# A later spread of two roots, another half-tile for twelve SwiGLU results, and a crossed order of blocks in two paired units

## The chip, the cores and the metric

The kernel runs on one core of one Trainium2 chip. The metric is the device time of one execution, in microseconds (us). The kernel before takes 1804.71 us, the median of 3 runs (1804.05 to 1805.07).

## What is computed

A trunk of two residual layers over 1024 positions of 1024 channels, in float32, conditioned by one vector `c`. Layer 0 mixes tokens with a causal convolution, layer 1 with trailing means over 2, 4, 8 and 16 positions. Behind each mixer stands a dense SwiGLU with 2816 hidden channels. Cut to what matters here:

```
for i in range(2):
    sh_m, sc_m, g_m, sh_f, sc_f, g_f = split(silu(c) @ ada_w[i] + ada_b[i], 6)
    h = rms_norm(x, norm_mix_g[i]) * (1 + sc_m) + sh_m
    x = x + (1 + g_m) * mixer_i(h)
    h = rms_norm(x, norm_ffn_g[i]) * (1 + sc_f) + sh_f
    x = x + (1 + g_f) * ((silu(h @ w_gate) * (h @ w_up)) @ w_down)
return rms_norm(x, final_g)
```

`rms_norm(x, g)` is `x * rsqrt(mean(x*x over channels) + 1e-6) * g`.

## The kernel before

**Layout.** Channels lie on the 128 partitions (8 tiles `x_0` to `x_7`), positions along the free dimension. The sequence is cut in two chunks of 512 positions, A and B. Their stages alternate, so that one chunk's norms and mixers lie beside the other's matrix products: layer 0's SwiGLU of A, then of B, then layer 1's of A, then of B.

**Products.** TensorE (PE) works with operands rounded to a shorter format. Each value is split in `hi` (a cast by ScalarE, ACT) and `lo` (the rest, a subtraction by VectorE, DVE), and each product is made of three: `hi` by the weights' `hi`, `lo` by `hi`, `hi` by `lo`. So a 1024-channel product of one hidden tile takes 8 x 3 matmuls. `hhi` and `hlo` are the parts of the normed input `h`; `ghi` and `glo` of the SwiGLU result; `thi` and `tlo` of sums of halves of `h` (below). Weights come as `raw` from memory, ACT makes the `hi` and, for some, DVE the `lo`.

**The order of the work.** A planner written in Python emits the program: it goes through a list of units (matrix work), keeps an estimated `clock` of each engine, and between them lets tasks take steps on the other engines. PE's order is what the planner emitted; the order on the other engines is then set by a scheduler that sees the whole program. A task that waits for an answer says so: `mean_rsqrt` (line 458) says "stats", issues 4 small products `var` (column sums of the squares over all channels), 12 small DVE steps for 1/sqrt, says "spread", and issues 4 products `rstd` that copy the row of roots onto all partitions. Then ACT copies the result to `ny`, DVE makes `t = x * gain * ny` for the 8 channel tiles, ACT makes `hhi` of each and DVE `hlo`. Behind "stats" and "spread" the planner leaves a number of microseconds by its clock (`DELAY`, line 62: 2.75 and 1.5 for urgent tasks) in which it emits matrix work of others. The norm ahead of layer 1's SwiGLU is the task "nf" (in `pooled`): chunk A's is placed in the last units of B's layer 0, chunk B's in the last units of A's layer 1. `Squares` beside it collects the squares.

**The paired units.** Most hidden tiles go in pairs, by a scheme of the Strassen kind: seven blocks of 12 products of 256 positions in place of eight (`ffn_pair`, line 1144). The blocks are named by their weights: `w11`, `w12`, `w22` as they are, `s1` to `s4` sums of them (the `shi`, `slo` of the rows below; each made by DVE or GpSimd and ACT in the slots of the weights). `w11`, `s2`, `s3` and `w22` accumulate one behind the other in the left half of a bank `a`; `w12` in the left half of a bank `e`; `s1` and `s4` in its right half. Since the partial results are wanted too, ACT copies `a` behind `w11` and again behind `s2` (to `r`, left and right), and the right half of `e` behind `s1` (to `q`). So `s2` waits for the first copy, `s3` for the second, `s4` for the copy of `q`. In most pairs the blocks run `w11, s1, s2, w12, s3, s4, w22`; in the first paired unit of A's and of B's layer 1 (`plain_first`) `w12` is taken ahead of `s1`, since the sums `t` of the norm's result are made only shortly before, and the order is `w11, w12, s1, s2, s3, s4, w22`. The seven sets of the pair behind it are prepared during the unit: a set is written when the block that read its slot is done.

**Tiles for the results.** `gslots` (line 252) hands out the tiles of `ghi` and `glo`, for each of a chunk's 22 hidden tiles in each of two layers. Tiles are 512 positions of 4 bytes in slots that are 32 elements (`ALIGN`, 128 bytes) longer; one of the two parts starts at the slot's start and the other 32 elements in, by turns, as the count `ch.made` says. In all, 176 such tiles are handed out. 12 of them, `ghi` and `glo` of A's layer 1 for the hidden tiles 0, 4, 8, 12, 16 and 20, start at 192 bytes past a multiple of 256; the other 164 start at 64.

Of the kernel before, what the change touches and what calls it, by code (L numbers as in the profile page):

```python
# [18 lines left out]
S = 1024  # L19
KT = D // P  # L20
F = 2816
NF = F // P
# [36 lines left out]
UNTIL = (18, 18, 22)  # L59
OUT_AT = 5  # L60
DELAY = {"stats": 2.75, "spread": 1.5}
DELAY_BEHIND = {"stats": 8, "spread": 4}

_COLS = {}
# [51 lines left out]
def trunk(ctx, tc, xT, c, vec, ada, adan, w1, w2, wgu, wdn, wpl, wph, out):  # L116
    nc = tc.nc
    ctx.enter_context(tc.manual_schedule(engines={mybir.EngineType.PE}))
    clock = {"PE": 0.0, "V": 0.0, "G": 0.0, "S": 0.0}
    V_ = Engine(nc.vector, "V", clock, PRICES["V"], lambda i: order(i))  # L120
# [53 lines left out]
    lax = [False]  # L174
# [37 lines left out]
    class Task:  # L212


        def __init__(self, gen, urgent=False, at=None):
            self.gen, self.done, self.urgent, self.until, self.mark = gen, False, urgent, 0.0, None
            tasks.insert(0 if urgent else len(tasks) if at is None else at, self)

        def step(self, e):
            if e != "V" or self.done or clock["PE"] < self.until and not forced[0]:  # L220
                return False
            try:
                if self.mark is None:
                    self.mark = clock["PE"] - V_.spent
                said = next(self.gen)
                if said == "wait":
                    return False
                if said in LOAD:
                    self.until = clock["PE"] + LOAD[said]
                    if said == "mean":  # L230
                        self.mark = None
                elif said is not None:
                    self.until = (self.mark + V_.spent if self.urgent else max(clock["V"], clock["S"])) + (DELAY if self.urgent or not lax[0] else DELAY_BEHIND)[said]
                    self.mark = None
            except StopIteration:
                self.done = True
                tasks.remove(self)
            return True
# [12 lines left out]

    def gslots(ch):

        odd = (ch.made // (KT // 2) + ch.i) % 2
        ch.made += 1
        return [wslot(ch, name, F32R, at * ALIGN, ch.n) for name, at in (("ghi", odd), ("glo", 1 - odd))]

# [886 lines left out]
    def ffn_pair(ch, l, me, following, downs, later, plain_first=False):  # L1144


        def emit(take):
            wt = take()
            wt.prepare()
            ws = wt.made  # L1150
            h, T = st["h", ch.i], st["T", ch.i]
            half = KT // 2
            b11 = [(hi[:, LEFT], lo[:, LEFT]) for hi, lo in h[:half]]
            b21 = [(hi[:, LEFT], lo[:, LEFT]) for hi, lo in h[half:]]
            b22 = [(hi[:, RIGHT], lo[:, RIGHT]) for hi, lo in h[half:]]
# [12 lines left out]
            left, right = e[:, LEFT], e[:, RIGHT]  # L1168
            r, q = temp(ch.n), temp(ch.n)
            quad(a[:, :H], w11, b11, True)  # L1170
            S_.copy(r[:, LEFT], a[:, :H])
            if plain_first:
                quad(left, w12, b21, True)
            quad(right, s1, t1, not plain_first)
            S_.copy(q[:, RIGHT], right)
            pace()
            down()
            quad(a[:, :H], s2, t2, False)
            S_.copy(r[:, RIGHT], a[:, :H])
            if following is not None and hasattr(following, "raws"):  # L1180
                following.prepare()
                st["ahead"]()
            if not plain_first:
                quad(left, w12, b21, False)
            if following is None:
                used[0] -= 2
                st["ahead"]()
            pace()
            down()
            quad(a[:, :H], s3, t3, False)  # L1190
            V_.tensor_tensor(q[:, RIGHT], q[:, RIGHT], a[:, :H], op=ADD)
            quad(right, s4, b22, False)
            V_.tensor_tensor(r, r, e, op=ADD)
            if later is not None:
                later.load(later.dps[0])
            pace()
            down()
            quad(a[:, :H], w22, t4, False)
            if me.which == 0:
                sg = st["sg", ch.i] = [window(ch.n, "sg") for _ in range(2)]  # L1200
                S_.activation(sg[0], r, AF.Silu)
                S_.activation(sg[1][:, RIGHT], q[:, RIGHT], AF.Silu, scale=-1.0)
                S_.activation(sg[1][:, LEFT], a[:, :H], AF.Silu, scale=-1.0)
            else:
                sg = st["sg", ch.i]
                V_.tensor_tensor(r, r, sg[0], op=MUL)
                V_.scalar_tensor_tensor(q[:, RIGHT], q[:, RIGHT], -1.0, sg[1][:, RIGHT], op0=MUL, op1=MUL)
                V_.scalar_tensor_tensor(q[:, LEFT], a[:, :H], -1.0, sg[1][:, LEFT], op0=MUL, op1=MUL)
                for i, t in enumerate((r, q)):
                    hi, lo = st["g", ch.i, me.f + i] = gslots(ch)  # L1210
                    S_.copy(hi, t)
                    V_.tensor_tensor(lo, t, f32(hi), op=SUB)
            pace()
            down()
            while downs is not None and downs.todo:
                downs.slot()
        return emit, (me,)
# [231 lines left out]
    st["taps", 0], st["taps", 1] = [False] * KT, [False] * KT  # L1449
    T = {}  # L1450

    def put(name, gen, urgent=False):
        def emit(take):
            T[name] = Task(gen(), urgent)
        unit(emit)

    def need(*names):
# [107 lines left out]
    def pooled(us, ch, out_at):  # L1565

        if ch.i == 0:
            ada_need((1, 0), (1, 1), (1, 2))
        put(("pool", ch.i), lambda: pool(ch))
        for i, (e, ws) in enumerate(us):  # L1570
            if i == out_at:
                need(("pool", ch.i))
                squares = Squares(ch)
                for q in range(2):
                    pool_out(ch, 1, q, squares)
                if ch.i == 0:
                    ada_need((1, 3), (1, 4), (1, 5))
                put(("nf", ch.i), lambda: norm(ch, 1, True, ("hn", ch.i), True, squares), True)
            unit(e, *ws)
        need(("nf", ch.i))  # L1580
        unit(lambda take: st.__setitem__(("h", ch.i), st["hn", ch.i]))
# [88 lines left out]
```

## Time and profile before

| | |
|---|---|
| time, median of 3 runs | 1804.71 us (1804.05 to 1805.07) |
| the profiled execution's own time | 1806.63 us |
| its span in the profile | 1804.9 us |
| mean granted TensorE clock | 0.993 |
| PE busy | 1769.9 us, 98% of the span |
| DVE, ACT and GpSimd (POOL) busy | 1401.4, 1044.5 and 549.5 us |

Times in the profile are microseconds from the start of the span. A row of a timeline gives the start, the duration, the engine, the line of the kernel, the operation, what it writes and reads (without the numbers that tell equally named tiles apart), shapes, a count, and in brackets how long the engine had been idle before and what released it. Matmuls overlap, so the distance from one start to the next says more than the duration. Since every operation is recorded by a helper, nearly all rows have the helper's line: L132 for matmuls, L110 for the other engines.

### The profile page before, as it was taken

What the parts mean: (1) busy time and instruction counts of PE and PEld (TensorE: products, weight loads), DVE (VectorE), ACT (ScalarE), POOL (GpSimd) and SP (SyncE); (2) the same over time, 40 slices, a digit from 0 to 9 for tenths busy, and PEclk for the clock granted to TensorE, in tenths of its full rate; (3) what the DMA queues carried; (4) which work ended last, traced back from release to release, by engine and by line L of the source; (5) the groups of instructions that cost most, each with busy time, mean ns of one, the idle gap of its engine ahead of it and who ended that gap; (6) DMA issues with size and microseconds to landing.
All of it is one profiled execution on the core that took longest, in us unless ns stands there. A gap on an engine that the chain in (4) does not pass through costs nothing.

```text
span 1804.9 us, 27284 instructions
## 1 busy us (share of the span) xinstructions
PE 1769.9 (98%) x10148; PEld 1536.0 (85%) x10148; DVE 1401.4 (78%) x2278; ACT 1044.5 (58%) x1682; POOL 549.5 (30%) x600
## 2 busy tenths in 40 slices
PE   9999998999999999999999999999999999999997
PEld 7777777888888888899998878999998789999996
DVE  8689846978775328989996988878769888887866
ACT  4776765776746455555556356555554556555553
POOL 0389723887734121211113501101125111011111
PEclk9999999999999999999999999999999999999998
DMA  9969676998978998877665566455555665655441
GB/s 305 283 181 264 170 168 166 238 220 209 233 205 209 233 216 201 233 203 205 201 186 146 147 155 153 129 133 140 136 128 145 166 150 137 184 141 138 127 111 57
DMA packets 113207, 322.88 MB, mean 179 GB/s; under 512 B 11057, under 2 KB 21425, under 8 KB 113074
## 3 DMA queue, kind: packets, MB, share of 16 engines
q1 hardware_dynamic: 77936, 222.56, 37.3%
q0 software_dynamic: 33984, 97.53, 30.2%
q8 instruction: 79, 1.29, 0.3%
q10 hardware_dynamic: 1154, 1.05, 0.2%
q14 instruction: 54, 0.44, 0.1%
HBM read 316.90 MB, written 4.19 MB: 178 GB/s over the span
## 4 chain that ended last, share of the span: by engine, by line
PE 88%; DVE 3%; issue 3%; DMA 2%; ACT 2%; POOL 1%; POOLq 0%; SPq 0%; DVEq 0%; ACTq 0%
PE dn L132 25%; PE up L132 24%; PE gate L132 24%; PE y L132 5%; PE a L132 3%; PE g L132 2%; PE first L132 2%; DVE x L110 1%; ACT w L110 1%; PE ada L132 1%; PE idle L132 1%; DMA w<-in_wdn_dram 1%; ACT t L110 1%; PE rstd L132 1%; DMA raw<-in_wgu_dram 0%
## 5 line engine op out<-in xcount | busy, mean ns | idle before, releaser
L132 PE MATMUL dn<-ghi,w 128*128 128x512 f32 (+1 forms) x1440 | 474.7, 388 | 0.8 <-ACT t L110 0.6
L110 ACT CAST w<-raw 128x512 fp32r<-128x512 f32 (+1 forms) x410 | 320.4, 783 | 168.4 <-PE up L132 73.3
L132 PEld LDWEIGHTS dn<-ghi,w 128*128 128x128 f32 x1440 | 269.2, 189 | 51.4 <-ACT t L110 1.0
L110 DVE SCALAR_TENSOR_TENSOR x<-dn,gains,x 128x512 f32<-128x512 f32 (+1 forms) x360 | 262.9, 736 | 63.0 <-PE dn L132 57.5
L110 ACT ACTIVATE w<-raw 128x1024 fp32r<-128x1024 f32 (+1 forms) x236 | 206.9, 877 | 172.6 <-PE dn L132 50.2
L1095 POOL DMA_DIRECT2D w<-in_wgu_dram x100 | 87.0, 873 | 637.3 <-PE up L132 206.1
L132 PE MATMUL dn<-glo,w 128*128 128x512 f32 (+1 forms) x720 | 279.4, 388 | 0.1
L132 PE MATMUL up<-hhi,w 128*128 128x512 f32 (+1 forms) x1008 | 274.9, 347 | 0.0
L132 PE MATMUL gate<-hhi,w 128*128 128x512 f32 (+1 forms) x1008 | 274.9, 347 | 0.0
L110 POOL TENSOR_TENSOR pa<-pa,pr 128x512 f32<-128x512 f32 x174 | 240.5, 1480 | 41.2 <-ACT pr L110 38.1
L132 PEld LDWEIGHTS gate<-hhi,w 128*128 128x128 f32 x1008 | 179.6, 189 | 26.0 <-PE ada L132 0.4
L132 PEld LDWEIGHTS up<-hhi,w 128*128 128x128 f32 x1008 | 179.7, 189 | 24.6
L132 PE MATMUL gate<-hlo,w 128*128 128x512 f32 (+1 forms) x504 | 175.0, 347 | 0.0
L132 PE MATMUL up<-hlo,w 128*128 128x512 f32 (+1 forms) x504 | 174.8, 347 | 0.0
L110 DVE SCALAR_TENSOR_TENSOR ca<-u,vecs,ca 128x512 f32<-128x512 f32 x246 | 171.7, 748 | 0.9
L110 DVE TENSOR_TENSOR w<-raw,w 128x512 fp32r<-128x512 f32 (+1 forms) x174 | 133.9, 775 | 31.9 <-ACT w L110 27.5
L132 PEld LDWEIGHTS dn<-glo,w 128*128 128x128 f32 x720 | 136.0, 189 | 20.9 <-POOL glo L110 0.6
L425 POOL DMA_DIRECT2D w<-in_wgu_dram x72 | 64.2, 891 | 246.7 <-ACT w L110 223.1
L110 ACT ACTIVATE pr<-u,vecs 128x512 f32<-128x512 f32 x174 | 118.4, 717 | 26.3 <-POOL pa L110 17.2
L110 DVE TENSOR_TENSOR t<-t,up 128x256 f32<-128x256 f32 (+1 forms) x88 | 53.7, 611 | 100.8 <-PE up L132 97.5
L110 ACT CAST shi<-ny 128x512 fp32r<-128x512 f32 x100 | 62.0, 620 | 119.2 <-PE gate L132 59.3
L132 PEld LDWEIGHTS gate<-hlo,w 128*128 128x128 f32 x504 | 95.2, 189 | 12.9 <-DVE hlo L110 0.2
(196 smaller groups left out, 3741.2 us busy)
## 6 DMA issues: line engine op xcount, KB each, us to landing
raw<-in_wgu_dram SPq DMA_DIRECT2D x176, 512.0 KB, 4.7
raw<-in_wdn_dram SPq DMA_DIRECT2D x88, 512.0 KB, 5.4
w<-in_wgu_dram POOLq DMA_DIRECT2D x72, 512.0 KB, 7.7
adaw<-in_ada_dram SPq DMA_DIRECT2D x64, 512.0 KB, 4.9
w<-in_wgu_dram POOLq DMA_DIRECT2D x100, 256.0 KB, 5.7
raw<-in_w_dram SPq DMA_DIRECT2D x42, 512.0 KB, 6.1
adaw<-in_adan_dram SPq DMA_DIRECT2D x32, 512.0 KB, 6.1
w<-in_w_dram POOLq DMA_DIRECT2D x32, 512.0 KB, 8.2
```

What stands on the lines that cost most here:

```text
L110: self.last = self.order(getattr(self.eng, name)(out, *args, **kw))
L132: last_mm[0] = nc.tensor.matmul(out, lhsT, rhs, start=start, stop=stop, **kw).ins.name
L425: order(nc.gpsimd.dma_start(as_src(lo), src, accum_op=ADD))
L1095: order(nc.gpsimd.dma_start(lo, src, accum_op=ADD))
```

## The change

There are three edits. In the changed kernel the helpers stand one line lower (L133, L111).

1. The task "nf" gets its own delays, `DELAY_AMONG`: "spread" is 4.2 by the planner's clock in place of 1.5.
2. In `gslots`, `turned` swaps the places of `ghi` and `glo` within their slots for the hidden tiles 0, 4, 8, ... of chunk A's layer 1. Addresses change, and no instruction or wait. With it all 176 tiles start at 64 bytes past a multiple of 256.
3. In `ffn_pair` with `plain_first`, the order of blocks is `w11, w12, s2, s1, s3, s4, w22`.

```diff
+DELAY_AMONG = {"stats": 2.75, "spread": 4.2}
...
-                    self.until = (self.mark + V_.spent if self.urgent else max(clock["V"], clock["S"])) + (DELAY if self.urgent or not lax[0] else DELAY_BEHIND)[said]
+                    self.until = (self.mark + V_.spent if self.urgent else max(clock["V"], clock["S"])) + (self.delay or (DELAY if self.urgent or not lax[0] else DELAY_BEHIND))[said]
...
-        odd = (ch.made // (KT // 2) + ch.i) % 2
+        turned = ch.i == 0 and ch.made >= NF and (ch.made - NF) % 4 == 0
+        odd = (ch.made // (KT // 2) + ch.i + turned) % 2
...
+            def crossed(first):
+                quad(right, s1, t1, first)
+                S_.copy(q[:, RIGHT], right)
+
             if plain_first:
                 quad(left, w12, b21, True)
-            quad(right, s1, t1, not plain_first)
-            S_.copy(q[:, RIGHT], right)
+            else:
+                crossed(True)
             pace()
             down()
             quad(a[:, :H], s2, t2, False)
...
-            if not plain_first:
+            if plain_first:
+                crossed(False)
+            else:
                 quad(left, w12, b21, False)
...
-                put(("nf", ch.i), lambda: norm(ch, 1, True, ("hn", ch.i), True, squares), True)
+                put(("nf", ch.i), lambda: norm(ch, 1, True, ("hn", ch.i), True, squares), True, delay=DELAY_AMONG)
```

**The root on PE.** PE's order where chunk A's "nf" spreads its root, among the last `dn` products of B's layer 0 (`dn_9901` is the second block of 6 products behind the column sums `var`). Before:

```order
L132 MATMUL dn_9901<-ghi_9644,w_9730 128x512
L132 MATMUL rstd_9909<-ident,col_9881 128x128 [waits DVE_49]
L132 MATMUL rstd_9909<-ident,col_9881 128x128 x3
L132 MATMUL dn_9948<-ghi_9407,w_9722 128x512
L132 MATMUL dn_9948<-glo_9408,w_9722 128x512
```

and in the changed kernel, where two further blocks stand ahead (`dn_9917` is the fourth) and `gate_9979` opens the next unit:

```order
L133 MATMUL dn_9917<-ghi_9644,w_9730 128x512
L133 MATMUL rstd_9925<-ident,col_9881 128x128 [waits DVE_49]
L133 MATMUL rstd_9925<-ident,col_9881 128x128 x3
L133 MATMUL dn_9964<-ghi_9407,w_9722 128x512
L133 MATMUL dn_9964<-glo_9408,w_9722 128x512
L133 MATMUL dn_9964<-ghi_9407,w_9723 128x512
L133 MATMUL dn_9964<-ghi_9644,w_9729 128x512
L133 MATMUL dn_9964<-glo_9645,w_9729 128x512
L133 MATMUL dn_9964<-ghi_9644,w_9730 128x512
L133 MATMUL gate_9979<-hhi_5913,w_9779 128x512 [waits Activation_49]
```

The spread moved from 12 to 24 products behind the column sums, and from 18 to 6 products ahead of the next unit. In B's "nf" the same two blocks of 6 change sides.

**The norm on ACT.** ACT's order from the copy of that root (`ny`) on; `hhi_9835` to `hhi_9849` are the `hi` parts of the 8 channel tiles, `w_9975` to `w_10114` steps on weights. Before:

```order
L110 COPY ny_9914<-rstd_9909 128x512 [waits PE_49]
L110 ACTIVATE hhi_9835<-t_9916,mod 128x512 [waits DVE_49]
L110 ACTIVATE hhi_9837<-t_9920,mod 128x512 [waits DVE_49]
L110 ACTIVATE w_9975<-raw_9972 128x1024 [waits PE_49]
L110 ACTIVATE hhi_9839<-t_9924,mod 128x512 [waits DVE_49]
L110 CAST w_9983<-raw_9981 128x1024 [waits DMAHW1_49,DMASW4_49,PE_49]
L110 ACTIVATE w_9984<-raw_9981 128x1024 [waits PE_49]
L110 CAST w_10045<-raw_10043 128x1024 [waits DMAHW2_49,DMASW5_49,PE_49]
L110 ACTIVATE hhi_9841<-t_9928,mod 128x512 [waits DVE_49]
```

and in the changed kernel the same stretch:

```order
L111 COPY ny_9930<-rstd_9925 128x512 [waits PE_49]
L111 ACTIVATE w_9975<-raw_9972 128x1024 [waits PE_49]
L111 CAST w_9983<-raw_9981 128x1024 [waits DMAHW1_49,DMASW4_49,PE_49]
L111 ACTIVATE w_9984<-raw_9981 128x1024 [waits PE_49]
L111 CAST w_10045<-raw_10043 128x1024 [waits DMAHW2_49,DMASW5_49,PE_49]
L111 ACTIVATE hhi_9835<-t_9932,mod 128x512 [waits DVE_49]
L111 ACTIVATE hhi_9837<-t_9936,mod 128x512 [waits DVE_49]
L111 ACTIVATE hhi_9839<-t_9940,mod 128x512 [waits DVE_49]
```

Four weight steps of 1024 columns moved ahead of the first `hhi`. Further on, `hhi_9847` and `hhi_9849` moved behind the weight step `w_10114` and the silu `t_10038` of the running unit.

**The norm on DVE.** DVE's last steps of the same norm; `hlo_9848` and `hlo_9850` belong to the seventh and eighth channel tile. Before:

```order
L110 SCALAR_TENSOR_TENSOR hlo_9846<-t_9936,mod,hhi_9845 128x512 [waits Activation_49]
L110 SCALAR_TENSOR_TENSOR hlo_9848<-t_9940,mod,hhi_9847 128x512 [waits Activation_49]
L110 TENSOR_TENSOR hf_10121<-hhi_9843,hlo_9844 128x512 [waits DVE_49]
L110 TENSOR_TENSOR hf_10160<-hhi_9837,hlo_9838 128x512
L110 SCALAR_TENSOR_TENSOR hlo_9850<-t_9944,mod,hhi_9849 128x512 [waits Activation_49]
```

and in the changed kernel:

```order
L111 SCALAR_TENSOR_TENSOR hlo_9846<-t_9952,mod,hhi_9845 128x512 [waits Activation_49]
L111 TENSOR_TENSOR w_10052<-raw_10049,w_10051 128x1024 [waits DMAHW3_49,PE_49]
L111 TENSOR_TENSOR hf_10121<-hhi_9843,hlo_9844 128x512 [waits DVE_49]
L111 TENSOR_TENSOR hf_10160<-hhi_9837,hlo_9838 128x512
L111 TENSOR_TENSOR t_10038<-t_10038,up_9980 128x512 [waits PE_49,Activation_49]
L111 SCALAR_TENSOR_TENSOR hlo_9848<-t_9956,mod,hhi_9847 128x512 [waits Activation_49]
L111 SCALAR_TENSOR_TENSOR hlo_9850<-t_9960,mod,hhi_9849 128x512 [waits Activation_49]
```

A step on weights, two sums `hf` and the multiply of the running unit's result now stand ahead of `hlo_9848`.

**The paired unit.** PE's order in A's first paired unit where the second block on bank `a` (`gate_10364`) ends and the third begins; `shi_10348` is `s2`, `shi_10354` is `s3`, `slo_10343` is of `s1`. Before:

```order
L132 MATMUL gate_10364<-thi_10298,shi_10348 128x256
L132 MATMUL gate_10364<-tlo_10299,shi_10348 128x256
L132 MATMUL gate_10364<-thi_10298,slo_10349 128x256
L132 MATMUL gate_10364<-thi_10133,shi_10354 128x256 [waits Activation_49]
L132 MATMUL gate_10364<-tlo_10134,shi_10354 128x256
```

and in the changed kernel, with bank `e` as `gate_10365`:

```order
L133 MATMUL gate_10365<-thi_10298,shi_10342 128x256
L133 MATMUL gate_10365<-tlo_10299,shi_10342 128x256
L133 MATMUL gate_10365<-thi_10298,slo_10343 128x256
L133 MATMUL gate_10364<-thi_10133,shi_10354 128x256 [waits Activation_49]
L133 MATMUL gate_10364<-tlo_10134,shi_10354 128x256
```

The block `s1` came between `s2` and `s3`. 12 products on, the first of `s4` (`gate_10365<-hhi_9843,shi_10360`) now waits for ACT too, which it did not before. On ACT the two copies change places. Before:

```order
L110 CAST shi_10432<-acc_10430 128x512 [waits PE_49,Activation_49]
L110 COPY t_10367<-gate_10365 128x256 [waits PE_49,Activation_49]
L110 CAST w_10562<-raw_10456 128x512 [waits DMAHW4_49,DMASW4_49]
L110 ACTIVATE w_10562<-raw_10456 128x512
L110 CAST shi_10438<-ny_10436 128x512 [waits PE_49]
L110 COPY t_10366<-gate_10364 128x256 [waits PE_49]
```

and in the changed kernel:

```order
L111 CAST shi_10419<-acc_10417 128x512 [waits PE_49,Activation_49]
L111 COPY t_10366<-gate_10364 128x256 [waits PE_49]
L111 CAST w_10562<-raw_10443 128x512 [waits DMAHW4_49,DMASW4_49]
L111 ACTIVATE w_10562<-raw_10443 128x512
L111 CAST shi_10425<-ny_10423 128x512 [waits PE_49]
L111 COPY t_10367<-gate_10365 128x256 [waits PE_49,Activation_49]
```

The copy of `a` (`t_10366`, the tile `r`) now goes first, and the copy of `e` (`t_10367`, `q`) four steps behind it.

More of the change, by code (lines that the diff above doesn't have):

```diff
@@ L212, in trunk, with __init__ @@
     class Task:
-        def __init__(self, gen, urgent=False, at=None):
+        def __init__(self, gen, urgent=False, at=None, delay=None):
+            self.delay = delay
             self.gen, self.done, self.urgent, self.until, self.mark = gen, False, urgent, 0.0, None
@@ L1450, in trunk, with put @@
     T = {}
-    def put(name, gen, urgent=False):
+    def put(name, gen, urgent=False, **kw):
         def emit(take):
-            T[name] = Task(gen(), urgent)
+            T[name] = Task(gen(), urgent, **kw)
         unit(emit)
```

## The prediction

> **What bounds the kernel now.** I read the page first, for the share of each engine:
>
> ```profile
> span 1804.9 us, 27284 instructions
> ...
> PE 1769.9 (98%) x10148; PEld 1536.0 (85%) x10148; DVE 1401.4 (78%) x2278; ACT 1044.5 (58%) x1682; POOL 549.5 (30%) x600
> ```
>
> PE is busy for all but 35.0 us of the span. So an edit gains only where it lets PE start sooner or makes a product shorter, and all other engines count through PE's waits. The second view is PE's waits by releaser (total, times, longest):
>
> ```profile
> PE rstd L132 <- DVE col L110: 8.3, 6, 2.5
> ...
> PE gate L132 <- ACT t L110: 2.6, 2, 1.3
> ```
>
> The first row holds the waits of the root products `rstd` for their DVE chain, 6 of them; two are those of the task "nf". The second row holds the two waits of the first paired units, 1.3 us each. The third view is PE's timeline at both.
>
> **The change part by part. The root (edit 1).** PE's timeline at A's "nf", and B's row:
>
> ```profile
> 1042.23 0.39 PE L132 MATMUL dn<-ghi,w 128*128 128x512 f32 x1
> 1042.69 1.05 PE L132 MATMUL var<-ones,acc 128*128 128x1 f32 x8
> 1043.61 0.47 PE L132 MATMUL dn<-ghi,w 128*128 128x512 f32 x1
> ...
> 1046.23 0.39 PE L132 MATMUL dn<-ghi,w 128*128 128x512 f32 x1
> 1047.94 1.16 PE L132 MATMUL rstd<-ident,col 128*128 128x128 f32 x8 [1.32 <-DVE col L110]
> ...
> 1053.05 0.39 PE L132 MATMUL gate<-hhi,w 128*128 128x512 f32 x1
> ...
> 1413.24 1.16 PE L132 MATMUL rstd<-ident,col 128*128 128x128 f32 x8 [1.32 <-DVE col L110]
> ```
>
> 12 `dn` products from 1043.61 to 1046.23 take 0.23 each after the first, so the 13th could start at 1046.46. Changing to the small fp32 products takes 0.23 more (1042.23 to 1042.69 is 0.46 for one product), so unhindered `rstd` would start at 1046.69. It starts at 1047.94: 1.25 us lost, and B's row shows the same wait. With 12 further products ahead (12 x 0.227 = 2.72) PE comes to `rstd` at 1049.41, when DVE's column has been there since about 1047.9. The wait goes, the six blocks stand all the same, and the next unit's first gate product comes at 1053.05 - 1.25 = 1051.80. Gain 1.25 at each place, 2.5 in all.
>
> What is late next: `rstd` itself is 1.47 us later (1049.41 against 1047.94), and on ACT four weight steps now stand between `ny` and the first `hhi`. ACT's and DVE's rows there:
>
> ```profile
> 1049.13 0.59 ACT L110 COPY ny<-rstd 128x512 f32<-128x512 f32 x1 [8.59 <-PE rstd L132]
> ...
> 1052.34 1.06 ACT L110 ACTIVATE w<-raw 128x1024 fp32r<-128x1024 f32 x1 [0.41 <-PE dn L132]
> 1053.31 0.70 ACT L110 ACTIVATE hhi<-t,mod 128x512 fp32r<-128x512 f32 x1
> 1053.92 1.03 ACT L110 CAST w<-raw 128x1024 fp32r<-128x1024 f32 x1
> 1054.86 1.05 ACT L110 ACTIVATE w<-raw 128x1024 fp32r<-128x1024 f32 x1
> ```
>
> ```profile
> 1053.07 0.74 DVE L110 SCALAR_TENSOR_TENSOR hlo<-t,mod,hhi 128x512 fp32r<-128x512 f32 x1
> 1053.73 0.75 DVE L110 SCALAR_TENSOR_TENSOR x<-dn,gains,x 128x512 f32<-128x512 f32 x1
> ...
> 1057.04 0.69 DVE L110 TENSOR_TENSOR hf<-hhi,hlo 128x512 f32<-128x512 f32 x1
> ...
> 1059.62 1.22 DVE L110 TENSOR_TENSOR w<-raw,w 128x1024 fp32r<-128x1024 f32 x1
> 1060.76 0.75 DVE L110 SCALAR_TENSOR_TENSOR hlo<-t,mod,hhi 128x512 fp32r<-128x512 f32 x1
> ```
>
> `ny` follows `rstd` by 1.19 us, so it starts at 1050.60 and leaves ACT at about 1051.1. Two activations at 0.97 and two casts at 0.94 are 3.82: the first `hhi` starts at 1054.92 and ends 0.70 later, at 1055.62, where it was at 1050.54 before. DVE can then do its `hlo`. By the order, DVE has from there to the seventh tile's `hlo`: 10 scalar-tensor-tensor steps at 0.66 (1053.07 to 1053.73), 4 tensor steps of 512 at about 0.60 (0.69 less the same overlap of 0.09) and 2 weight steps at 1.14 (1059.62 to 1060.76), together 11.28. So that `hlo` starts at about 1066.94 and is done at 1067.69. PE's row that reads it:
>
> ```profile
> 1068.23 0.39 PE L132 MATMUL gate<-hlo,w 128*128 128x512 f32 x1
> ```
>
> PE would come there at 1068.23 - 1.25 = 1066.98. So it waits 0.7 us, and with a slow first product behind the wait (0.11, below) loses about 0.85. The eighth tile is ready 0.66 later and PE wants it 0.68 later, so one wait covers both. Net gain 0.4 per place, 0.8 for both; the ends are 2.5 (the scheduled steps run in gaps and nothing waits) and -0.5 (DVE 0.65 us later than laid out at each place). I take 0.8, since each term is a row, and only their gaps are mine.
>
> **The crossed blocks (edit 3).** PE's timeline at A's wait, and ACT's beside it:
>
> ```profile
> 1102.07 0.28 PE L132 MATMUL gate<-tlo,shi 128*128 128x256 f32 x1
> 1102.19 0.28 PE L132 MATMUL gate<-thi,slo 128*128 128x256 f32 x1
> 1103.78 0.39 PE L132 MATMUL gate<-thi,shi 128*128 128x256 f32 x1 [1.32 <-ACT t L110]
> 1104.01 0.28 PE L132 MATMUL gate<-tlo,shi 128*128 128x256 f32 x1
> ```
>
> ```profile
> 1101.53 0.37 ACT L110 COPY t<-gate 128x256 f32<-128x256 f32 x1
> ...
> 1102.32 0.63 ACT L110 ACTIVATE w<-raw 128x512 fp32r<-128x512 f32 x1
> 1102.85 0.61 ACT L110 CAST shi<-ny 128x512 fp32r<-128x512 f32 x1
> 1103.36 0.37 ACT L110 COPY t<-gate 128x256 f32<-128x256 f32 x1
> ```
>
> Products follow each other by 0.12 (1102.07 to 1102.19), so the second product of s3 should start at 1102.43; it starts at 1104.01. 1.58 us are lost, of which 0.11 is the slow first product (0.23 to the next, not 0.12). The reason is ACT: the copy that s3 waits for is the second in its row, behind two weight steps and a cast, at 1103.36.
>
> In the changed order the copy of `a` takes the first place (1101.53, done at 1101.90), and PE comes to s3 at 1102.31: no wait. The copy of `q` takes the place at 1103.36 and is done at 1103.73. It is wanted now, by s4, 12 products behind 1102.31, at 1103.74. PE started 0.05 behind the copy's end before (1103.73 to 1103.78), so s4 loses 0.04 and a slow first product of 0.11: 0.15. Gain 1.58 - 0.15 = 1.43 at A, and the same at B by the equal wait in the second view: 2.85. Ends: 3.2 if nothing is left of the wait, and 1.8 if one more ACT cast (0.53, 1102.32 to 1102.85) comes ahead at each place.
>
> Who else waits: the multiply of the running unit, now ahead of the seventh `hlo`, reads products that end earlier than before. The sums `t` of the paired unit hang on the norm, and come about 0.5 us later on DVE. Their last row:
>
> ```profile
> 1098.07 0.69 DVE L110 TENSOR_TENSOR tlo<-tf,thi 128x512 fp32r<-128x512 f32 x1
> ```
>
> It ends at 1098.76, and s3, which reads it first, stood at 1103.78. These 5 us cover it, less the 1.5 that s3 comes sooner; past them it would cost what it is late.
>
> **The half-tiles (edit 2).** The windows of the `dn` products that read `ghi` and `glo`, PE's busy time (and number) of those products alone, in stretches where one pair's products lie:
>
> ```profile
> 1111.00:1142.00 31.00, 12.54 (x48) 1.00 0.46 121
> 1142.20:1173.50 31.30, 12.38 (x48) 1.00 0.52 141
> ...
> 1298.60:1329.40 30.80, 12.54 (x48) 1.00 0.57 143
> 1354.40:1371.10 16.70, 16.65 (x72) 1.00 0.74 184
> 1440.00:1451.30 11.30, 11.19 (x48) 1.00 0.55 121
> 988.80:1005.20 16.40, 16.35 (x72) 1.00 0.82 161
> 1074.70:1085.80 11.10, 10.99 (x48) 1.00 0.56 125
> ```
>
> A's layer 1 alternates between 12.54 and 12.38 from pair to pair, from the first window of these to the third row, four pairs at 12.54, and these are the pairs with hidden tiles 0, 4, 8 and 12, whose tiles start at 192 past a multiple of 256. The granted clock is 1.00 in all. Tiles 16 and 20 lie in the stretches of 16.65 and 11.19; the same stretches of B's layer 0, with all tiles at 64, take 16.35 and 10.99. So the start costs 4 x 0.16 + 0.30 + 0.20 = 1.14, all of it PE time. No instruction moves, so nothing hides it: gain 1.1, ends 0 and 1.15.
>
> The Trainium skill has a rule that speaks against this edit: "SBUF — State Buffer", section "SBUF: two separate sides", says that PE never waits on anyone for its port and names one contended port pair alone, that of VectorE and GpSimd; by it a start shifted by 128 bytes changes nothing here and the sum loses 1.1. The trace of before does not agree, with 12.54 against 12.38, but it cannot show that the start address is the reason.
>
> **The sum.** 0.8 + 2.85 + 1.1 = 4.75. The profiled execution of 1806.63 with a span of 1804.9 would come to 1801.9 and 1800.15. It lies 1.9 above the median; against the median I predict 1804.71 - 4.75 = 1800.0, rounded.
>
> **Rivals.**
>
> *The root's gain stays whole.* DVE would have to reach the seventh `hlo` 0.7 us sooner than laid out, for instance because its `t` steps are done while ACT has not yet made the first `hhi`, and so I count too many of them behind it. Then 2.5 in place of 0.8, 6.45 in all: 1798.3. Against it speaks that ACT's four weight steps are certain by the order. Chance 0.17.
>
> *The start address does nothing*, and the alternation has another reason. 3.65 in all: 1801.1. For it: only A's layer 1 shows it in the trace, so the tiles' start is not separated from the place in the program. Chance 0.13. The skill's rule above would have this outcome.
>
> *The wait returns at s4.* ACT's weight steps between the two copies wait for their load; if it lands 1 us late at each unit, the copy of `q` is late one for one and s4 waits. 4.75 - 2 = 2.75: 1802.0. In before the steps ran without a gap between 1101.53 and 1103.36, against it. Chance 0.12.
>
> *Slower: the late `hhi` behind a load.* On ACT the seventh and eighth `hhi` now stand behind a weight cast that waits for its own transfer. SP's row of the issue, and the page's row of such issues with the median time to landing:
>
> ```profile
> 1053.43 2.84 SPq L420 DMA_DIRECT2D raw<-in_wgu_dram  x2
> ...
> raw<-in_wgu_dram SPq DMA_DIRECT2D x176, 512.0 KB, 4.7
> ```
>
> Issued at 1053.43 it lands at about 1058. The `hhi` is wanted by DVE at 1066.94; cast (0.94), silu and `hhi` (0.6 each, by 1053.31 to 1053.92) take 2.1, so it decides from a landing after about 1064.8, and from there PE's wait grows one for one, at a product that was never waited for before. To be slower by over 0.2% (3.61 us, about what a measurement of this kernel can tell from no change) the two places have to lose 4.75 + 3.6 = 8.4 us, 4.2 each: a landing 16 us behind the issue, which gives 1808.3. Chance 0.04.
>
> **How the numbers follow.** The forecast has 0.54. The likeliest case gives 1800.0. The range reaches to the whole root gain (1798.3) with 0.3 for the upper end of edit 3, and to the wait at s4 (1802.0) with 0.3 for the lower end of the root: 1798.0 to 1802.3. Some 0.15 is left out, the slower rival and the sums of two mishaps. Faster by over 0.2% means under 1801.1. That holds for most of the forecast (0.46 of its 0.54, the rest being its upper end), for the first rival, and for half of the second: 0.46 + 0.17 + 0.07, and 0.04 for a late load of less than half a microsecond: 0.74. Same takes the rest but for the slower rival, 0.22; slower 0.04.
>
> **What would show it.** In the changed profile: no row `rstd` with a wait for `col` near 1049 and 1414; a wait of `gate` for DVE's `hlo` of about 0.7 at the seventh tile's products in each of the two units behind; `ny` some 1.5 later; no wait at s3 and one of about 0.05 at s4; `dn` windows of A's layer 1 all at 12.38, 16.35 and 11.0. Wrong would make it: a wait that is left at `rstd`, `gate` waits over 1.25 at either unit (edit 1 then costs), waits at s4 over 1 us, or `dn` windows that still alternate.

## The result and the profile after

The changed kernel takes 1800.76 us, the median of 20 runs (1797.65 to 1803.68), beside 1805.7 us for the kernel before in 20 runs on the same chips. The ratio is 0.9971, with a 95% interval of 0.9964 to 0.9977: 4.2 to 6.5 us less, 5.2 in the middle. Forecast were 4.75 less, 1800.0 us, and a range of 1798.0 to 1802.3. The profiled execution has a span of 1799.0 us, 5.9 below that of before. The page's head and the rows of PE's waits that changed:

```profile
span 1799.0 us, 27291 instructions
...
PE 1768.0 (98%) x10148; PEld 1535.9 (85%) x10148; DVE 1400.3 (78%) x2278; ACT 1043.0 (58%) x1682; POOL 549.2 (31%) x600
```

```profile
PE rstd L133 <- DVE col L111: 6.0, 4, 2.7
...
PE gate L133 <- DVE hlo L111: 1.2, 2, 0.6
```

Two waits at `rstd` are gone (4 of 6 are left, 6.0 us of 8.3). Both waits of `gate` for ACT's copy are gone from the list. A new row has come, two waits of 0.6 of `gate` for `hlo`. (The list counts idle time behind a product's modelled end, so a start that is a tenth or two late doesn't appear in it; the timelines below show those.)

**The root.** PE at A's "nf", from the column sums to the next unit:

```profile
1042.46 1.05 PE L133 MATMUL var<-ones,acc 128*128 128x1 f32 x8
1043.37 0.48 PE L133 MATMUL dn<-ghi,w 128*128 128x512 f32 x1
...
1048.71 0.39 PE L133 MATMUL dn<-ghi,w 128*128 128x512 f32 x1
1048.94 1.05 PE L133 MATMUL rstd<-ident,col 128*128 128x128 f32 x8
1049.74 0.48 PE L133 MATMUL dn<-ghi,w 128*128 128x512 f32 x1
...
1051.22 0.39 PE L133 MATMUL gate<-hhi,w 128*128 128x512 f32 x1
```

From the first `dn` to the first `gate` it is now 7.85 us, and was 9.44: 1.59 gained. `rstd` follows the last `dn` by 0.23, without any time for the change of operand. ACT and DVE behind it, and the product that has to wait:

```profile
1050.03 0.59 ACT L111 COPY ny<-rstd 128x512 f32<-128x512 f32 x1 [9.34 <-PE rstd L133]
1050.51 1.07 ACT L111 ACTIVATE w<-raw 128x1024 fp32r<-128x1024 f32 x1
1051.47 1.04 ACT L111 CAST w<-raw 128x1024 fp32r<-128x1024 f32 x1
1052.41 1.06 ACT L111 ACTIVATE w<-raw 128x1024 fp32r<-128x1024 f32 x1
1053.36 1.04 ACT L111 CAST w<-raw 128x1024 fp32r<-128x1024 f32 x1
1054.30 1.95 ACT L111 ACTIVATE hhi<-t,mod 128x512 fp32r<-128x512 f32 x3
```

```profile
1055.06 1.41 DVE L111 SCALAR_TENSOR_TENSOR hlo<-t,mod,hhi 128x512 fp32r<-128x512 f32 x2 [1.01 <-ACT hhi L111]
...
1066.37 1.41 DVE L111 SCALAR_TENSOR_TENSOR hlo<-t,mod,hhi 128x512 fp32r<-128x512 f32 x2
```

```profile
1065.96 0.61 PE L133 MATMUL gate<-hhi,w 128*128 128x512 f32 x2
1067.17 0.50 PE L133 MATMUL gate<-hlo,w 128*128 128x512 f32 x1 [0.59 <-DVE hlo L111]
1067.51 0.63 PE L133 MATMUL gate<-hhi,w 128*128 128x512 f32 x2
```

The four weight steps fill ACT from 1050.51 to 1054.30; DVE idles 1.01 us for the first `hhi`, and 11.31 us after it begins the seventh `hlo`. It is done at about 1067.1, and PE, which could have started at 1066.41, starts at 1067.17, 0.76 later (0.59 of it is idle time in the profile's count); the next product follows by 0.34 in place of 0.23. So 0.9 is lost.

**The paired unit.** PE from the end of `s1` over the end of `s3` to `s4`, and ACT's two copies with what stands between them:

```profile
1101.27 0.28 PE L133 MATMUL gate<-thi,slo 128*128 128x256 f32 x1
1101.39 0.28 PE L133 MATMUL gate<-thi,shi 128*128 128x256 f32 x1
...
1102.68 0.28 PE L133 MATMUL gate<-thi,slo 128*128 128x256 f32 x1
1102.87 0.39 PE L133 MATMUL gate<-hhi,shi 128*128 128x256 f32 x1
1103.09 0.28 PE L133 MATMUL gate<-hlo,shi 128*128 128x256 f32 x1
```

```profile
1100.62 0.36 ACT L111 COPY t<-gate 128x256 f32<-128x256 f32 x1
1100.88 0.62 ACT L111 CAST w<-raw 128x512 fp32r<-128x512 f32 x1
...
1101.93 0.61 ACT L111 CAST shi<-ny 128x512 fp32r<-128x512 f32 x1
1102.44 0.37 ACT L111 COPY t<-gate 128x256 f32<-128x256 f32 x1
```

No product in `s3` comes out of step. The first of `s4` starts 0.19 behind its forerunner and its successor 0.22 behind it, where the step is 0.12: 0.17 lost. The copy of `q` ends at 1102.81 and PE starts 0.06 later. At B the first of `s4` starts 0.25 behind its forerunner (1465.11 to 1465.36), so a little more is lost there.

**The `dn` windows** of A's layer 1, in the columns of before:

```profile
1108.00:1139.00 31.00, 12.38 (x48) 1.00 0.47 127
1139.20:1170.50 31.30, 12.38 (x48) 1.00 0.52 140
...
1295.60:1326.40 30.80, 12.39 (x48) 1.00 0.57 145
1351.20:1367.90 16.70, 16.26 (x72) 1.00 0.76 186
1436.50:1447.90 11.40, 10.87 (x48) 1.00 0.54 116
```

The alternation is gone; the seven windows of pairs lie at 12.38 or 12.39.

**Where the time went.** PE's starts of the same products in the two traces, subtracted, give the gain of each stretch. The table has them for all profiles of this study, each against that of before (negative is sooner; "t" is the start in the trace of before):

| stretch (t of its ends) | changed | e1 | e2 | e3 | e4 | e5 | e6 | e7 | e8 | e9 | e10 |
|---|---|---|---|---|---|---|---|---|---|---|---|
| start to layer 0's SwiGLU (0 to 300.1) | 0.16 | -1.30 | -1.44 | -1.43 | -0.39 | 2.15 | -2.53 | -1.91 | 1.68 | 1.53 | 1.07 |
| layer 0, no edit (300.1 to 1010.6) | -0.02 | 0.03 | -0.02 | 0.03 | 0.04 | 4.44 | 0.01 | 0.01 | -0.03 | 0.00 | -0.01 |
| A's root (1042.69 to 1069.37) | -0.70 | -0.70 | -0.03 | -0.04 | -1.40 | -0.60 | -0.72 | -1.34 | -0.07 | -0.69 | -1.37 |
| A's paired unit (1096.57 to 1108.17) | -1.41 | 0.01 | 0.18 | -1.23 | -1.37 | -1.39 | -1.30 | -1.11 | -0.46 | -1.19 | -1.21 |
| A's pairs, `dn` (1111.04 to 1371.03) | -0.74 | 0.00 | -0.73 | 0.02 | -0.74 | 0.25 | 0.59 | -0.73 | 0.00 | -0.51 | -0.74 |
| B's root (1408.03 to 1434.67) | -0.69 | -0.67 | 0.04 | 0.03 | -1.36 | -0.54 | -0.57 | -1.33 | 0.03 | -0.67 | -1.37 |
| A's last `dn` (1434.67 to 1451.24) | -0.25 | 0.02 | -0.25 | 0.01 | -0.26 | 0.06 | 0.01 | -0.22 | 0.00 | -0.25 | -0.25 |
| B's paired unit (1451.24 to 1473.74) | -1.38 | 0.00 | 0.10 | -1.42 | -1.44 | -1.43 | -1.27 | -1.31 | -0.46 | -1.40 | -1.33 |
| B's other pairs, no edit (1473.74 to 1786.38) | -0.04 | -0.04 | -0.01 | 0.02 | -0.04 | 1.12 | -0.04 | -0.04 | -0.01 | -0.04 | -0.04 |

The six stretches of the edits give 5.17 for the changed kernel. The rest of the 5.9 is no part of the change. One piece, 0.37 between 1010.61 and 1042.69, is a wait of 0.26 with its slow restart, for a transfer, that the profile of before has (`dn` for `w<-in_wdn_dram`) and none of the eleven others, those without an edit there included. The other, 0.46, is how fast one row of `rstd` products near the end went by (1.01 us from 1792.33 to the next product in before, 0.55 in the changed kernel), which differs between two profiles of one kernel (0.00 in e4, 0.47 in e10). The first row shows what a single time is worth here: up to 2.5 us either way before any edit, so the effects of single edits are read from the stretches. These have a scatter of their own: "changed" and e9, two profiles of one kernel, differ by up to 0.23 in them.

### The profile page after: what moved, and what is told of

Same layout as the page of the kernel before. It is cut to its first block, busy times and chain, and to the rows that moved or that the text cites. A ratio compares the mean times of both kernels' runs of the same rounds, so it can differ in the third digit from the quotient of the medians.

```text
span 1799.0 us, 27291 instructions
## 1 busy us (share of the span) xinstructions
PE 1768.0 (98%) x10148; PEld 1535.9 (85%) x10148; DVE 1400.3 (78%) x2278; ACT 1043.0 (58%) x1682; POOL 549.2 (31%) x600
## 4 chain that ended last, share of the span: by engine, by line
PE 91%; DVE 3%; issue 2%; ACT 2%; DMA 1%; POOL 1%; POOLq 0%; SPq 0%; ACTq 0%; DVEq 0%
PE dn L133 26%; PE up L133 25%; PE gate L133 24%; PE y L133 5%; PE a L133 3%; PE g L133 2%; PE first L133 2%; ACT w L111 1%; PE ada L133 1%; PE idle L133 1%; DVE t L111 1%; DVE hlo L111 1%; PE rstd L133 1%; DVE x L111 1%; DMA adaw<-in_adan_dram 1%
## 5 line engine op out<-in xcount | busy, mean ns | idle before, releaser
L133 PE MATMUL dn<-ghi,w 128*128 128x512 f32 (+1 forms) x1440 | 474.2, 387 | 0.6 <-ACT t L111 0.6
L111 ACT CAST w<-raw 128x512 fp32r<-128x512 f32 (+1 forms) x410 | 320.4, 783 | 170.0 <-PE up L133 72.9
L133 PEld LDWEIGHTS dn<-ghi,w 128*128 128x128 f32 x1440 | 269.4, 189 | 50.5 <-ACT t L111 1.0
L111 DVE SCALAR_TENSOR_TENSOR x<-dn,gains,x 128x512 f32<-128x512 f32 (+1 forms) x360 | 262.3, 734 | 63.8 <-PE dn L133 56.5
L111 ACT ACTIVATE w<-raw 128x1024 fp32r<-128x1024 f32 (+1 forms) x236 | 206.9, 877 | 170.9 <-PE dn L133 49.3
L133 PE MATMUL dn<-glo,w 128*128 128x512 f32 (+1 forms) x720 | 279.3, 388 | 0.1
L133 PE MATMUL up<-hhi,w 128*128 128x512 f32 (+1 forms) x1008 | 275.1, 347 | 0.0
L133 PE MATMUL gate<-hhi,w 128*128 128x512 f32 (+1 forms) x1008 | 275.0, 348 | 0.0
L111 POOL TENSOR_TENSOR pa<-pa,pr 128x512 f32<-128x512 f32 x174 | 240.6, 1481 | 41.2 <-ACT pr L111 38.1
L133 PEld LDWEIGHTS gate<-hhi,w 128*128 128x128 f32 x1008 | 179.7, 189 | 25.7 <-ACT hhi L111 0.4
L133 PEld LDWEIGHTS up<-hhi,w 128*128 128x128 f32 x1008 | 179.8, 189 | 24.5
L133 PE MATMUL gate<-hlo,w 128*128 128x512 f32 (+1 forms) x504 | 175.3, 348 | 1.2 <-DVE hlo L111 1.2
L133 PE MATMUL up<-hlo,w 128*128 128x512 f32 (+1 forms) x504 | 175.0, 347 | 0.0
L111 DVE SCALAR_TENSOR_TENSOR ca<-u,vecs,ca 128x512 f32<-128x512 f32 x246 | 171.6, 746 | 0.9
L111 DVE TENSOR_TENSOR w<-raw,w 128x512 fp32r<-128x512 f32 (+1 forms) x174 | 133.6, 773 | 32.0 <-ACT w L111 27.5
L133 PEld LDWEIGHTS dn<-glo,w 128*128 128x128 f32 x720 | 136.1, 189 | 20.4 <-POOL glo L111 0.6
L111 ACT ACTIVATE pr<-u,vecs 128x512 f32<-128x512 f32 x174 | 118.4, 717 | 26.3 <-POOL pa L111 17.2
L111 ACT CAST shi<-ny 128x512 fp32r<-128x512 f32 x100 | 62.0, 620 | 119.9 <-PE gate L133 59.7
L111 DVE TENSOR_TENSOR t<-t,up 128x256 f32<-128x256 f32 (+1 forms) x88 | 53.6, 609 | 99.6 <-PE up L133 96.4
L133 PEld LDWEIGHTS gate<-hlo,w 128*128 128x128 f32 x504 | 95.3, 189 | 15.0 <-DVE hlo L111 2.2
```

Source lines behind the costliest of these rows:

```text
L111: self.last = self.order(getattr(self.eng, name)(out, *args, **kw))
L133: last_mm[0] = nc.tensor.matmul(out, lhsT, rhs, start=start, stop=stop, **kw).ins.name
```

## Experiments

**e1, e2, e3: each edit alone**, that is the kernel before with one part of the diff.

> Edit 1 alone (the root spread 24 products behind its sums; tiles and block order as before). Theory (the terms add, each has its own place): the wait at rstd goes at both places, which moves the next unit 1.6 us forward; the seventh tile's hlo is late by 0.6 on DVE and costs 0.9 with the slow product behind it; net 0.7 at each place, 1.4 in all, ratio to before 0.9992. Rival (the new wait comes from the three edits together): no wait of gate for hlo, 3.2 us gained, ratio 0.9982. The waits at s3 (1.3 each) and the alternation of the dn windows (12.54 and 12.38) stay.

Measured 1802.93 us in 11 runs, ratio 0.9994 (0.9984 to 1.0003), which alone doesn't tell it from no change; the stretches do, 0.70 and 0.67 at the roots and 0 elsewhere. PE's waits:

```profile
PE gate L133 <- ACT t L111: 2.7, 2, 1.3
...
PE gate L133 <- DVE hlo L111: 1.2, 2, 0.6
```

The new wait comes from edit 1 alone. The rival falls.

> Edit 2 alone (only the start addresses of 12 tiles differ from the kernel before). Theory (the start address is the cause): all four slow windows of A's layer 1 come to 12.38, and about 1.0 us is gained, ratio 0.9994. Rival (the windows changed because edits 1 and 3 moved what lies beside the products): the windows alternate as before, and the time is that of before within 0.2 us in the profile. Waits at rstd and at s3 as before.

Measured 1803.58 us in 11 runs, ratio 0.9993 (0.9984 to 1.0002). The two `dn` stretches became 0.73 and 0.25 shorter. The first two windows of pairs, which are 12.54 and 12.38 in before:

```profile
1109.00:1140.00 31.00, 12.38 (x48) 1.00 0.47 124
1140.20:1171.50 31.30, 12.38 (x48) 1.00 0.53 142
```

With not one instruction moved the first window is 0.16 shorter by its busy time, and about 0.12 by the starts of its products. The start address is the cause; the rival falls. (The wait at `s3` was 1.5 at the longest in place of 1.3; e9 below shows why it moves.)

> Edit 3 alone. Theory: s3 doesn't wait, s4 loses 0.17 to a wait of 0.05 and a slow first product; 1.4 us gained in each of the two units, 2.8 in all, ratio 0.9984. Rival (the copy of q meets the weight steps of ACT at another time when the root isn't moved): s4 waits about 0.5 or more at each unit, and 1.8 or less is gained, ratio 0.9990 or more.

Measured 1803.02 us in 11 runs, ratio 0.9984 (0.9975 to 0.9993). The units gained 1.23 and 1.42. No row of `gate` waiting for ACT is left. `s4` at A:

```profile
1101.61 0.28 PE L132 MATMUL gate<-thi,slo 128*128 128x256 f32 x1
1101.97 0.39 PE L132 MATMUL gate<-hhi,shi 128*128 128x256 f32 x1
1102.20 0.27 PE L132 MATMUL gate<-hlo,shi 128*128 128x256 f32 x1
```

Here it loses 0.35, with 0.36 and 0.23 in place of 0.12, so in this profile the copy of `q` came about 0.17 later than in the changed kernel. The theory holds, with that much play. The three ratios multiplied are 0.9971, that of all three edits together; with intervals of 0.0009 either way, the last digit is luck.

**e4: 18 products behind the sums.** The planner's delay for "spread" is cut by a third:

```diff
-DELAY_AMONG = {"stats": 2.75, "spread": 4.2}
+DELAY_AMONG = {"stats": 2.75, "spread": 2.8}
```

> All three edits, but the root is spread 18 products behind its sums in place of 24. ACT's order then has the first hhi directly behind ny, ahead of the weight steps. Theory (the late root and the four weight steps ahead of the first hhi cause the new wait): rstd comes when the column is just done and loses 0.1 to 0.3, the first hhi starts about 4 us sooner, gate doesn't wait for hlo; 0.6 better than the changed kernel at each place, 1.2 in all, 6.4 below before by the terms (5.2 for the changed kernel), ratio 0.9965. Rival (DVE's own work of 11.3 us ahead of the seventh hlo is the bound): gate still waits 0.5 or more for hlo, and the time is that of the changed kernel or above. Second rival (the column is late at 18): rstd waits over 0.5, no better than the changed kernel.

Measured 1799.04 us in 5 runs, ratio 0.9962 (0.9950 to 0.9975). PE at A's root, and ACT behind it:

```profile
1046.65 0.39 PE L133 MATMUL dn<-ghi,w 128*128 128x512 f32 x1
1047.00 1.16 PE L133 MATMUL rstd<-ident,col 128*128 128x128 f32 x8
```

```profile
1048.19 0.59 ACT L111 COPY ny<-rstd 128x512 f32<-128x512 f32 x1 [7.99 <-PE rstd L133]
1049.60 0.72 ACT L111 ACTIVATE hhi<-t,mod 128x512 fp32r<-128x512 f32 x1 [0.82 <-DVE t L111]
1050.23 1.04 ACT L111 ACTIVATE w<-raw 128x1024 fp32r<-128x1024 f32 x1
```

The column is just done: `rstd` follows by 0.35, not 0.23. The first `hhi` starts 1.4 behind `ny` (4.3 in the changed kernel), and PE's list has no row of `gate` for `hlo`. Each root is worth 1.40 and 1.36, twice the changed kernel's. The theory holds, and both rivals fall.

**e7: the weight steps behind the second `hhi`**, with the root at 24 products. Scheduling edges put each weight cast behind it:

```diff
         S_.activation(hi, t, AF.Identity, bias=sh)
+        if ffn and l == 1 and k == 1:
+            held_nf[0] = S_.last.ins.name
...
         S_.copy(hi, raw)
+        if held_nf[0] is not None:
+            tc.add_manual_dep(S_.last.ins, held_nf[0], edge, reason="behind the normed tiles")
```

> The changed kernel with the root at 24 products, but ACT's weight steps are ordered behind the second hhi of the norm. Theory (the weight steps ahead of the first hhi make the new wait): first hhi at about 1.3 behind ny in place of 4.3, the seventh hlo starts about 1.5 sooner, gate doesn't wait for it, 0.9 better than the changed kernel at each place, 1.8 in all. Rival 1 (the late root itself makes the wait): gate waits 0.5 or more for hlo as in the changed kernel. Rival 2 (the weights come late instead): a new wait of DVE or PE for w, and no gain.

Measured 1797.99 us in 4 runs, ratio 0.9951 (0.9935 to 0.9968); the stretch ahead of any edit is 2.1 better than the changed kernel's in this profile, so the roots tell: 1.34 and 1.33. ACT, and the late product at A:

```profile
1047.81 0.59 ACT L111 COPY ny<-rstd 128x512 f32<-128x512 f32 x1 [10.11 <-PE rstd L133]
1049.22 1.39 ACT L111 ACTIVATE hhi<-t,mod 128x512 fp32r<-128x512 f32 x2 [0.82 <-DVE t L111]
```

```profile
1065.01 0.50 PE L133 MATMUL gate<-hlo,w 128*128 128x512 f32 x1
1065.35 0.39 PE L133 MATMUL gate<-hhi,w 128*128 128x512 f32 x1
```

The seventh tile is in time; the eighth is 0.14 late and costs 0.26 with the slow next step. 0.64 of the 0.9 is back with the weight steps alone, at an unchanged place of the root. So they make most of the wait. The theory's 0.9 was too much, and the first rival's 0.5 and more did not come. The second rival came in small: in each of the two units DVE now waits 0.29 for a weight step of ACT (before its `w` at 1055.37 and 1417.49), where the changed kernel's DVE had no such wait in these units. That alone is more than the 0.14 by which the eighth tile is late, but the late root and the eighth tile's place behind a multiply on DVE could also make it, and this run doesn't separate them.

**e8: ACT's queue without the crossing.** The kernel before, with an edge that puts the two weight steps behind the copy of `r`:

```diff
-                low_by_dma(a22, *w22, self.srcs[1][:, BACK])
+                low_by_dma(a22, *w22, self.srcs[1][:, BACK], after_copy[0])
```

> The kernel before (none of the three edits), but in the first paired units the two weight steps that stand on ACT between the copy of q and the copy of r are ordered behind the copy of r. PE's order stays w11, w12, s1, s2, s3, s4, w22. Theory (ACT's queue is half of the wait at s3, the way from PE to ACT and back the other half, which only the crossing hides): the copy starts 0.37 behind the start of s2's last product and takes 0.37, s3 starts about 0.8 sooner at each unit, a wait of 0.5 is left; 1.6 gained in all, against 2.8 for the crossing. Rival (the queue is all of it): no wait left, 2.8 gained.

Measured 1805.31 us in 10 runs, ratio 0.9993 (0.9983 to 1.0002). The median doesn't tell it from no change; by the stretches the units gain 0.46 each. ACT, and PE's first product of `s3`:

```profile
1103.42 0.62 ACT L110 CAST shi<-ny 128x512 fp32r<-128x512 f32 x1 [0.49 <-PE gate L132]
1103.95 0.36 ACT L110 COPY t<-gate 128x256 f32<-128x256 f32 x1
```

```profile
1104.36 0.39 PE L132 MATMUL gate<-thi,shi 128*128 128x256 f32 x1 [0.86 <-ACT t L110]
```

The expected 0.8 was wrong: one more step stands ahead of the copy, the cast `shi`, which is itself released by the end of `s2` (it writes into the slot that `s2` read) and takes 0.53 in front of the copy. So of 1.58 lost, the two weight steps are 0.46, and the chain from `s2` over cast and copy back to PE is the rest. Of what was tried, only the block in between hides that. Ordering this cast behind the copy as well was not tried; by the rows it would bring `s3` up to 0.53 forward.

**e5 and e6: other starts.** e5 starts all 176 tiles at 192 past a multiple of 256; e6 starts those of A's layer 1 for all even hidden tiles there.

```diff
-        odd = (ch.made // (KT // 2) + ch.i + turned) % 2
+        odd = (ch.made // (KT // 2) + ch.i + turned + 1) % 2
```

```diff
-        turned = ch.i == 0 and ch.made >= NF and (ch.made - NF) % 4 == 0
+        turned = ch.i == 0 and ch.made >= NF and (ch.made - NF) % 4 == 2
```

> The changed kernel, but in A's layer 1 the swap falls on the hidden tiles 2, 6, 10, 14, 18, so that these and the tiles 0, 4, 8, ... both start at 192. Theory (a start at 192 is slow, wherever it stands): all dn windows of A's layer 1 come to 12.54, about 1.8 to 2.2 us slower than the changed kernel by the windows. Rival (only the places of the pairs 0, 4, 8, ... in the program are slow): windows alternate as before or stay at 12.38.

Its first two windows of pairs:

```profile
1106.00:1137.00 31.00, 12.50 (x48) 1.00 0.48 124
1137.20:1168.50 31.30, 12.50 (x48) 1.00 0.51 140
```

All seven windows of pairs are slow, at 12.50 to 12.54. The stretch of A's pairs is 0.59 longer than before, 1.33 longer than in the changed kernel, and the last `dn` 0.26: 1.6, a little under the theory's 1.8 to 2.2. Its time of 1799.91 (one run) doesn't show that, as the stretch ahead of any edit was 2.7 quicker. The place in the program has no part.

> The changed kernel with the places of ghi and glo swapped in every slot: all 176 tiles start at 192 past a multiple of 256, none at 64. Theory (each product that reads a tile at 192 is longer): 0.16 us for 24 products in a paired window and up to 0.39 for 24 in the last ones are 6.7 to 16 ns each; with 2160 dn products 14 to 35 us slower than the changed kernel, and every dn window of a pair at about 12.7. Rival 1 (the cost lies in a change between the two starts within one accumulation): no change, as all tiles are alike; windows at 12.38. Rival 2 (the start has no part): windows at 12.38 as well.

Measured 1808.45 us in 10 runs, ratio 1.0011 (1.0002 to 1.0021). The same two windows:

```profile
1115.50:1146.50 31.00, 12.46 (x48) 1.00 0.48 123
1146.70:1178.00 31.30, 12.43 (x48) 1.00 0.53 140
```

A start at 192 is slower wherever it stands: 4.4 us in layer 0, which has no other edit. Added up against the changed kernel, layer 0 (4.46), the two `dn` rows of the table (0.99 and 0.31) and B's other pairs (1.16) give 6.9, and the last `dn` products of B's layer 0, between A's root and its paired unit, another 0.35: 7.3, not 14 to 35. A window with the tiles of both hidden tiles at 192 takes 0.05 to 0.08 more than with none, one with those of one of the two takes 0.12 to 0.16 more. So the theory's direction holds and its size fails: in these windows two hidden tiles at 192 cost less than one at 192 beside one at 64. The rival that only the change of start costs fails too, as it gave 0. Both seem to play, and why either does is not settled by these runs.

**e9 and e10: the changed kernel and e4 once more, side by side.**

> The changed kernel itself, beside the next on the same chip. From the start of layer 0's SwiGLU to the end its profile should be 6.1 us below that of the kernel before, as in its first profile; ratio 0.9971 or near.

> The changed kernel with the root 18 products behind its sums, a second time, beside the changed kernel. Theory (rstd without a wait and no wait of gate for hlo): root places 1.4 each in place of 0.7, so 1.4 us below the changed kernel from layer 0's SwiGLU to the end, and a ratio to before lower by 0.0008. Rival (the first profile's difference is that of two executions): the stretches around the two roots differ by less than 0.3 from those of the changed kernel.

Measured 1801.64 us in 11 runs, ratio 0.9980 (0.9971 to 0.9989), and 1799.25 us in 6 runs, ratio 0.9966 (0.9953 to 0.9978). From layer 0's SwiGLU to the start of the last root product, e9 is 5.9 below before, and e10 7.4. The roots are 0.69 and 0.67 in e9, 1.37 and 1.37 in e10: the difference is the root's, and the rival falls. The version with 18 products is the best of the study by the stretches, 1.4 us below the changed kernel at the two roots; by the medians it is 1.7 and 2.4 below, with intervals that overlap. (e7 has the lowest median, 1797.99 in 4 runs, but its stretches gain less than those of e4 and e10.)

e9, the same program as "changed", also shows a longer wait at A's `s4`: its first product starts 0.42 behind its forerunner, where the step is 0.12 and the first profile had 0.19.

```profile
1103.88 0.28 PE L133 MATMUL gate<-thi,slo 128*128 128x256 f32 x1
1104.30 0.39 PE L133 MATMUL gate<-hhi,shi 128*128 128x256 f32 x1
```

ACT starts the weight step behind the first of its two copies at A 0.26 to 0.27 behind that copy's start in before and in the changed kernel's first profile, but 0.45 to 0.57 behind it in e2, e3, e7, e9 and e10. In e7 the timeline names what released that step, the transfer of `raw`, with 0.20 of idle time; in the other four the idle time is too short to be listed. So the second copy comes 0.2 to 0.3 later where that load lands late, and whoever waits for it, `s4` or in the old order `s3`, pays.

## Why the prediction was right

- **The bound.** PE stayed at 98%, and the time moved by what PE's waits and products moved. This was right.
- **Edit 1, the gain at the root.** Forecast 1.25 at each place, measured 1.6. The working's step "changing to the small fp32 products takes 0.23 more" is mis-sized: before `rstd` the change costs nothing (1048.71 to 1048.94), and behind an unwaited `rstd` the next product comes 0.80 later, not 0.91. I had taken the 0.23 from `var`, where it stands in both traces.
- **Edit 1, the new wait.** Forecast a wait of 0.7 at the seventh tile and 0.85 lost; measured by the starts 0.76 and 0.9. DVE's work from its first `hlo` to the seventh was summed to 11.28 and took 11.31. (The sum 1055.62 + 11.28 is 1066.90, not 1066.94; it changes nothing.) The 0.34 that the root gained beyond the forecast brought `ny` and the whole chain on DVE forward as well as PE, so the wait kept its size. e7 shows that the four weight steps are most of it. Net 0.4 forecast, 0.7 measured at each place, 1.4 for both in place of 0.8, inside the bounds given.
- **Edit 3.** Forecast 1.43 at A and 2.85 in all, measured 1.41 and 1.38; a loss of 0.15 at `s4` forecast, 0.17 measured at A. e8 adds what the trace of before didn't tell me: taking ACT's two weight steps away would have been worth a third as much.
- **Edit 2.** Forecast 1.1, measured 0.74 + 0.25, and the same in e2 alone. The mis-sized term is 4 x 0.16: the windows' busy time gives 0.16, but by the starts in e2 the four pairs gave 0.47 in all, with 0.27 for tile 16's stretch and 0.25 for tile 20's. The rule of the Trainium skill that the prediction weighed, "SBUF — State Buffer", section "SBUF: two separate sides", says that PE never waits on anyone for its port. Read as "placement costs PE nothing" it would have left the time as it was, and the trace disagrees with that reading: 12.54 against 12.38 for the same 48 products, with only addresses changed. It doesn't refute the rule itself, since no run shows that PE waits for another engine here, and it doesn't say which part of the chip is slower.
- **The sum.** 0.8 + 2.85 + 1.1 = 4.75 forecast, 1.4 + 2.8 + 1.0 = 5.2 measured; 0.6 more at the roots, less 0.15 at the other two, so the errors partly cancel. In absolute time the forecast of 1800.0 is 0.8 too low although the gain was larger than forecast, because the kernel before took 1805.7 in 20 runs and the forecast was set against 1804.71 from 3 runs.
- **The rivals.** The whole root gain did not come in the changed kernel, but came within 0.2 in e4. The start address did matter. The wait at `s4` returned in small: 0.07 at A and 0.13 at B in the changed profile, 0.30 at A in e9, of the same kernel. At A the cause is most likely the one that the rival named, ACT's weight step behind a late load (named by the timeline in e7), but it cost tenths and not 1 us. The late `hhi` stood behind its weight cast, which ended at about 1063.3, more than 3 us ahead of need.

## What to carry to other kernels

A product that depends on a short chain elsewhere should stand just as many products behind it as the chain needs: 12 left a wait, 18 left 0.1 us of one, and 24 moved the wait to the next consumer, mostly because weight steps filled ACT's queue ahead of it. Where two blocks of one accumulator are parted by a copy, the copy engine's queue ahead of it counts as much as the copy, and a block of another bank between them hid all but 0.1 to 0.5 us of both. Compare traces product by product: where single executions scatter by 2 us in stretches that no edit touches, six stretches of 0.2 to 1.4 us still came out alike to 0.3.

## What the runs showed of the hardware

- The start address of the moving operand's tile changes how long its products take: 512 positions of 4 bytes at 64 past a multiple of 256 bytes make a window of 48 products 12.38 us, with the tiles of one of its two hidden tiles at 192 past it 12.50 to 12.54, and with those of both at 192 12.43 to 12.46. No other start was tried, and the reason is open.
- The product behind one that waited comes late as well, in the waits shown here: 0.34 in place of 0.23 for 512 positions (1067.17 to 1067.51), and 0.22 to 0.23 in place of 0.12 for 256.
